# A hybrid SSD, pooling and gated-MLP block on one core: a low part behind dt's reading, row norm squares behind the panel's last put, and the last half stored in five chunks

## Chip, cores and metric

The kernel runs on one core of one Trainium2 chip. The metric is the device time of one execution in microseconds; the median over the runs is compared. Five engines work side by side, each through its own row of instructions in a fixed order: TensorE (PE; its weight loads are listed apart as PEld), VectorE (DVE), ScalarE (ACT), GpSimd (POOL) and SyncE (SP), which issues most of the DMAs.

## What is computed

One encoder block over 256 tokens of 2048 features in float32. Cut to what matters:

```python
hn = rmsnorm(h, mix_norm_pre)
z, xbc, dt_raw, u = jnp.split(hn @ w_in, split_at, axis=-1)     # 1024, 1536, 32, 1024 columns
y_ssd = ssd_mixer(z, xbc, dt_raw, ...)      # conv, softplus(dt_raw + dt_bias), a scan in both directions, gated by z
y_pool = pool_mixer(u, pool_w, pool_scale)  # centred means over 2, 4, 8, 16 tokens minus u, a linear map per group
h = h + rmsnorm(jnp.concatenate([y_ssd, y_pool], -1) @ w_out, mix_norm_post)

gate, val = jnp.split(rmsnorm(h, ffn_norm_pre) @ w_up, 2, axis=-1)          # 5632 columns each
ff = (gelu(dwconv_centred(gate, conv_w, conv_b)) * val) @ w_down
h = h + rmsnorm(ff, ffn_norm_post)

gate = sigmoid(rmsnorm(h, ple_norm_pre) @ w_ple_gate)
out = h + rmsnorm(gate * (p @ w_ple), ple_norm_post)
```

## The kernel before

**Matmuls in parts.** Each float32 operand is written as a sum of two parts in a shorter format, high and low, and a product is taken as high x high + high x low + low x high. `split` makes the parts of a weight tile: ACT casts the high part (line 151), VectorE subtracts it from the source to get the low one (line 152). `put` does so for activations, with a scale: ACT writes the high part (line 196), VectorE the low (line 197). All matmuls of such products are issued on line 87, so they are told apart by their tiles: the names `whi` and `wlo` at the end of a tile's name are the parts, the number ahead of them (0 or 1) is the half of a loaded 1 MB raw tile.

**Stages.** In order: `dtu` (dt and the pool branch's u, token-major, into three pairs of accumulators); `xbc` in slabs 2, 0, 1 (`feature_major`: four raw tiles each, two halves of 1024 columns, each half split and then multiplied); z, the scan and the pool mixer; `wo`, the output projection; the up projection of the MLP in 44 tiles, `ug` for gate and `uv` for value columns (`feature_pairs`, accumulators `ga` and `va`, of which a tile's first half goes high parts first and its second low parts first); the down projection `dn` in blocks, some of them by a scheme of seven products with sums stored to memory; the gate `gt` with the per-layer embedding `ple`, and the last addition and stores.

**Accumulators.** They live in PSUM. The pool `pmain` has six banks that the names take in turn, `pmisc` two. An accumulator of xbc takes a bank of dtu once that has been read out, in whichever order the pool hands them on. In the dtu stage each token half t is read by four instructions: dt on VectorE (line 540), u in three pieces on ACT (541), VectorE (542) and ACT (544). `rx` is the row factor of the first norm.

**What sets the order.** The code is recorded and its instructions are placed in each engine's row by a scheduler; `tc.issue_after(i)` puts what is recorded inside it behind instruction i in that order. Raw tiles (`raw`, four buffers) are loaded by SP (line 118) as soon as a buffer is free, so a load waits for the last reading of the tile four loads back. The dictionary `held` carries an instruction to the place where something is to be issued behind it. Before the change it is used in the up projection's first tile `ug00`, whose parts are made behind the panel's puts:

```python
behind = held.pop((name, u, j), None)
with tc.issue_after(behind) if behind else nullcontext():
    tiles.append(split(parts(f"{name}{u}_{j}"), r[:, j * 1024:(j + 1) * 1024], 0, 1024))
```

**Between wo and up.** `sublayer` ends by adding to the residual h in four column pieces; behind each piece `panel_part` transposes h on TensorE (`woxt`, line 383) and writes it back with `put` into the pages `wox`, which are the activations of up. Each page holds four of the sixteen feature blocks. Then `ple(0)` computes half of the embedding's product (`pl`, line 901), and `row_rstd("rf", h)` squares and sums each row half of h on ACT (`rfj`, line 399, 2048 columns), from which POOL makes the row factors `rf`. These are turned along the tokens by TensorE (`rfbp`) and multiplied in behind the first tiles of up.

**The end.** For the second token half, the last gate piece (`gtz`, 256 columns) is turned into a sum of squares; `rest_of` and `finish(1)` make the row factor `go1r` on POOL (line 1059), VectorE adds to h in four pieces of 512 columns (line 1064), and each is stored by SP (line 1066) as soon as it is done.

Of the kernel before, what the change touches and what calls it, by code (L numbers as in the profile page):

```python
# [11 lines left out]
F32 = mybir.dt.float32  # L12
F32R = mybir.dt.float32r
AF = mybir.ActivationFunctionType
ALU = mybir.AluOpType
# [36 lines left out]
def build(nc, a, out):  # L52
# [5 lines left out]
    with tile.TileContext(nc) as tc, \  # L58
# [9 lines left out]
        def ins(r):  # L68
            return getattr(r, "ins", r)

        def page(name, dtype=F32):
            return gp.tile([P, 2048], dtype, tag="pg", bufs=14, name=name)
# [4 lines left out]
        def tiny(name, n=2):  # L77
            return sp.tile([P, n], F32, tag="tiny", bufs=40, name=name)

        def main(name):  # L80
            return [pm.tile([P, 512], F32, tag="main", name=f"{name}_{i}") for i in range(2)]

        def misc(name):
            return pc.tile([P, 512], F32, tag="misc", name=name)

        def mm(o, lhsT, rhs, start, stop):
            last["pe"] = ins(nc.tensor.matmul(o, lhsT, rhs, start=start, stop=stop, skip_group_check=True))  # L87
# [16 lines left out]
        acc, acc2 = [main(f"dtu{t}") for t in range(2)], main("dtu2")  # L104
# [8 lines left out]
        last = {}  # L113
# [20 lines left out]
        def vec(i):  # L134
            return xt[0][:, i:i + 1] if i < V_SCW else vt[:, i - V_SCW:i - V_SCW + 1]


        spare, ready, held, stored = {}, {}, {}, {}

        def parts(name):  # L140

            if name in spare:
                return spare.pop(name)
            return [wp.tile([P, 1088], F32R, tag=tag, bufs=5, name=f"{name}{tag}") for tag in ("whi", "wlo")]

        def split(dst, src, c0, *cuts):

            hi, lo = dst
            for c1 in cuts:
                s = slice(c0, c1)  # L150
                last["act"] = ins(nc.scalar.copy(hi[:, s], src[:, s]))
                last["dve"] = ins(nc.vector.tensor_sub(lo[:, s], src[:, s], hi[:, s].bitcast(F32)))  # L152
                c0 = c1
            return hi, lo

        def raw(name, src, a_, b_):
            r = wp.tile([P, 2048], F32, tag="raw", bufs=4, name=name)
            last["dma"] = load(r[:, :a_ * b_].rearrange("p (a b) -> p a b", a=a_), src, True)
            return r
# [33 lines left out]
        def put(dst, src, scale):  # L193

            hi, lo = dst
            return (ins(nc.scalar.activation(hi, src, AF.Identity, scale=scale)),
                    ins(nc.vector.scalar_tensor_tensor(lo, src, scale, hi.bitcast(F32),
                                                       op0=ALU.mult, op1=ALU.subtract)))
# [3 lines left out]
        def aside():  # L202

            for job in (work.pop(0) if work else ()):
                job()
# [98 lines left out]
        def feature_major(name, w, c0, get, acc):  # L304

            for u in range(4):
                r = raw(f"{name}r{u}", w[c0 // 128 + u].unsqueeze(1), 1, 2048)
                tiles = []

                def step(j, kk, f):  # L310
                    k = 4 * u + 2 * j + kk
                    (wh, wl), (xh, xl) = tiles[j], get(k)
                    s = slice(kk * 512 + f * P, kk * 512 + (f + 1) * P)
                    for q, (ww, xx) in enumerate(((wh, xh), (wh, xl), (wl, xh))):
                        mm(acc[f // 2][:, f % 2 * L:(f % 2 + 1) * L], ww[:, s], xx,
                           k == 0 and q == 0 and f % 2 == 0, k == NK - 1 and q == 2)

                for j in range(2):
                    tiles.append(split(parts(f"{name}{u}_{j}"), r[:, j * 1024:(j + 1) * 1024], 0, 1024))
                    if u < 3:  # L320
                        for kk in range(2):
                            for f in range(4):
                                step(j, kk, f)
                if u == 3:
                    for f in range(4):
                        for j in range(2):
                            for kk in range(2):
                                step(j, kk, f)
                aside()
# [35 lines left out]
        def rms(name, parts, scale, n=1, base=EPS):  # L365

            for i, q in enumerate(parts):
                m = tiny(f"{name}m{i}", n)
                nc.gpsimd.tensor_scalar(m, q, scale, base, op0=ALU.mult, op1=ALU.add)
                base = m  # L370
            r = tiny(f"{name}r", n)
            nc.gpsimd.tensor_tensor(r, m, mhalf[:, :n], op=ALU.pow)
            last["mean"] = m
            return r

        def panel_part(name, pan, src, vcol, k0, k1):

            first = None
            for k in range(k0, k1, 2):
                ps = misc(f"{name}t{k}")  # L380
                for j in range(2):
                    for t in range(2):
                        nc.tensor.transpose(ps[:, (2 * j + t) * P:(2 * j + t + 1) * P],
                                            src[t][:, (k + j) * P:(k + j + 1) * P], ident)
                for j in range(2):
                    done = put(pan(k + j), ps[:, j * L:(j + 1) * L], vec(vcol + k + j))
                    last["put"] = done[1]
                    first = first or done
            return first

# [2 lines left out]
        def row_rstd(name, src):  # L393

            r = []
            for t in range(2):
                q = tiny(f"{name}q{t}", 1)
                junk = page(f"{name}j{t}")
                nc.scalar.activation(junk, src[t], AF.Square, accum_out=q)
                r.append(rms(f"{name}{t}", [q], 1.0 / D))  # L400
                means[name, t] = last["mean"]
            return r
# [60 lines left out]
        for u in range(0, NK, 2):  # L463
            r = [wp.tile([P, 2048], F32, tag="raw", bufs=4, name=f"dtur{u}") if u else r0, page(f"dtur{u + 1}")]
# [33 lines left out]
        with tc.issue_after(half[0]), tc.issue_after(half[1]):  # L498
# [3 lines left out]
            rx = row_rstd("rx", xs_)  # L502
# [35 lines left out]
        ut = page("u")  # L538
        for t in range(2):
            nc.vector.scalar_tensor_tensor(dt[:, t, :], acc[t][0][:, :32], rx[t], dtb, op0=ALU.mult, op1=ALU.add)  # L540
            nc.scalar.activation(ut[:, t * 1024:t * 1024 + 320], acc[t][0][:, 32:352], AF.Identity, scale=rx[t])  # L541
            nc.vector.tensor_scalar(ut[:, t * 1024 + 320:t * 1024 + 672], acc[t][1][:, :352], rx[t], None,
                                    op0=ALU.mult)
            nc.scalar.activation(ut[:, t * 1024 + 672:(t + 1) * 1024], acc2[t][:, :352], AF.Identity, scale=rx[t])
        rxb = along_tokens("rxb", rx)

# [230 lines left out]
        for t in range(2):  # L777
# [13 lines left out]
            r = rms(f"yn{t}", [ss], rz[t][:, 1:2], n=2)  # L791
# [103 lines left out]
        def ple(half):  # L895
            pl = page(f"pl{half}")
            acc = [main(f"ple{half}{t}") for t in range(2)]
            token_major(f"ple{half}", w_ple, half * 1024, [0, 1], lambda k: (pth[:, k, :], ptl[:, k, :]), acc)
            for t in range(2):
                for n in range(2):  # L900
                    nc.scalar.activation(pl[:, t * 1024 + n * 512:t * 1024 + (n + 1) * 512], acc[t][n],
                                         AF.Copy, scale=0.5)
            return pl
# [5 lines left out]
        h = [page(f"h{t}") for t in range(2)]  # L909
# [4 lines left out]


        pl = [ple(0)]
        rf = row_rstd("rf", h)
        for t in range(2):
            nc.gpsimd.tensor_scalar(fmean[t], means["rf", t], EPS, None, op0=ALU.mult)
        away = {n: dp.tile([P, 2048], F32, name=f"{n}_away") for n in ("h0", "h1", "pl0")}  # L920
# [112 lines left out]
        h = hb  # L1033
# [22 lines left out]
        def finish(t):  # L1056
            if t:
                r = tiny("go1r", 1)
                nc.gpsimd.tensor_tensor(r, sq[t][-1], mhalf[:, :1], op=ALU.pow)
            else:  # L1060
                r = rms("go0", sq[t], 1.0 / D)
            for c in range(4):
                s = slice(c * 512, (c + 1) * 512)
                nc.vector.scalar_tensor_tensor(vg[t][:, s], vg[t][:, s], r, h[t][:, s],
                                               op0=ALU.mult, op1=ALU.add)
                nc.sync.dma_start(out[t * P:(t + 1) * P, s], vg[t][:, s])

        for half in range(2):
            acc = [main(f"gt{half}{t}") for t in range(2)]
# [9 lines left out]
            for t in range(2):  # L1079
                for n, (o, c0) in enumerate(columns(acc[t])):  # L1080
                    c1 = c0 + o.shape[-1]
                    c = slice(half * 1024 + c0, half * 1024 + c1)
# [4 lines left out]
                    if end:  # L1087
# [3 lines left out]
                                                   op0=ALU.add, op1=ALU.mult)  # L1091
# [74 lines left out]
```

## Time and profile before

| | us |
|---|---|
| three runs | 1116.17, 1116.26, 1116.42 |
| median | 1116.26 |
| profiled execution | 1116.42 |
| its span, first to last instruction | 1114.6 |
| TensorE busy | 1102.3 (99%) |
| VectorE busy | 834.0 (75%) |
| ACT busy | 685.7 (62%) |
| mean granted TensorE clock | 0.997 |

The profile records one execution; its own time is 1.8 us more than its span. In the rows below a time is microseconds from the start of the span. A timeline row gives start, duration, engine, line, operation, output and inputs with the shape and the count, and in brackets the engine's idle time before it and what ended that. A row with a count above one groups neighbours of the same kind: its duration is that of the whole group. TensorE's matmuls overlap, so the spacing of their starts, not the duration of one, is what it needs for each.

### The profile page before, as it was taken

How to read it: one execution, taken by the hardware profiler on the slowest of the kernel's cores; microseconds unless marked ns; L12 is line 12 of the kernel's file. 1: busy time of each engine (PE TensorE's matmuls, PEld its weight loads, DVE VectorE, ACT ScalarE, POOL GpSimd, SP SyncE). 2: the span in 40 equal slices, each digit the busy share in tenths (PEclk: the TensorE clock that was granted, in tenths of full speed). 3: DMA queues.
4: the chain of work that ended last, by engine and by line, in shares of the span. 5: the costliest groups of instructions: out<-in, count | busy, mean ns of one | idle time of the engine just before them, and what ended most of it. 6: DMA issues, size and time to landing. Idle time of an engine off the chain costs nothing.

```text
span 1114.6 us, 15675 instructions
## 1 busy us (share of the span) xinstructions
PE 1102.3 (99%) x6040; PEld 963.5 (86%) x6040; DVE 834.0 (75%) x1047; ACT 685.7 (62%) x1006; POOL 53.0 (5%) x80
## 2 busy tenths in 40 slices
PE   9999999999999999999999999999999999999996
PEld 9999988888788888888888888888888888887885
DVE  6668888879786866767767677676788788897574
ACT  6757876555775565565655655556566466657462
POOL 0300023100200000000000000000000000001001
PEclk9999999999999999999999999999999999999998
DMA  9944445656576877777787687675788779875632
GB/s 354 376 174 150 154 151 212 242 210 224 212 282 252 304 262 249 280 259 253 280 290 253 239 323 253 213 253 220 253 312 296 265 275 348 308 253 209 247 131 75
DMA packets 48970, 275.68 MB, mean 247 GB/s; under 512 B 5248, under 2 KB 8192, under 8 KB 21632
## 3 DMA queue, kind: packets, MB, share of 16 engines
q1 hardware_dynamic: 48608, 274.33, 67.9%
q8 instruction: 47, 0.77, 0.3%
q10 hardware_dynamic: 288, 0.36, 0.1%
q14 instruction: 27, 0.22, 0.1%
HBM read 251.86 MB, written 22.81 MB: 246 GB/s over the span
## 4 chain that ended last, share of the span: by engine, by line
PE 92%; DMA 3%; ACT 2%; issue 1%; DVE 1%; POOL 0%; SPq 0%; POOLq 0%; DVEq 0%; ACTq 0%
PE va L87 22%; PE ga L87 21%; PE dna L87 15%; PE gt L87 7%; PE woa L87 7%; PE xbc L87 6%; PE dns L87 5%; PE z L87 4%; DMA dtur<-w_dtu 2%; DMA x<-x 1%; PE wos L87 1%; PE yd L87 1%; PE pw L87 1%; PE ple L87 0%; PE seg L87 0%
## 5 line engine op out<-in xcount | busy, mean ns | idle before, releaser
L87 PE MATMUL ga<-wox,ug_0whi 128*128 128x512 f32 x352 | 87.7, 391 | 0.0
L87 PE MATMUL va<-wox,uv_0whi 128*128 128x512 f32 x352 | 87.6, 391 | 0.0
L87 PE MATMUL ga<-wox,ug_1whi 128*128 128x512 f32 x352 | 87.2, 389 | 0.0
L87 PE MATMUL va<-wox,uv_1whi 128*128 128x512 f32 x352 | 86.9, 389 | 0.0
L87 PEld LDWEIGHTS va<-wox,uv_1whi 128*128 128x128 f32 x352 | 66.1, 188 | 13.7
L87 PEld LDWEIGHTS ga<-wox,ug_1whi 128*128 128x128 f32 x352 | 66.0, 188 | 13.7
L87 PEld LDWEIGHTS va<-wox,uv_0whi 128*128 128x128 f32 x352 | 64.6, 188 | 12.4
L87 PEld LDWEIGHTS ga<-wox,ug_0whi 128*128 128x128 f32 x352 | 64.6, 188 | 12.3
L87 PE MATMUL ga<-wox,ug_1wlo 128*128 128x256 f32 x352 | 49.7, 283 | 0.9 <-DVE ug_1wlo L152 0.9
L87 PE MATMUL ga<-wox,ug_0wlo 128*128 128x256 f32 x352 | 49.5, 283 | 0.0
L87 PE MATMUL va<-wox,uv_1wlo 128*128 128x256 f32 x352 | 49.4, 283 | 0.0
L87 PE MATMUL va<-wox,uv_0wlo 128*128 128x256 f32 x352 | 49.2, 283 | 0.0
L87 PEld LDWEIGHTS ga<-wox,ug_0wlo 128*128 128x128 f32 x352 | 46.8, 191 | 1.8
L87 PEld LDWEIGHTS va<-wox,uv_0wlo 128*128 128x128 f32 x352 | 46.7, 191 | 1.7
L87 PEld LDWEIGHTS ga<-wox,ug_1wlo 128*128 128x128 f32 x352 | 45.4, 192 | 1.3 <-DVE ug_1wlo L152 1.3
L87 PEld LDWEIGHTS va<-wox,uv_1wlo 128*128 128x128 f32 x352 | 45.4, 192 | 0.0
L877 POOL TENSOR_SCALAR dnm<-dnq,fmean 128x1 f32<-128x1 f32 x2 | 0.6, 282 | 586.8 <-ACT dnj L874 586.8
L87 PE MATMUL xbc<-hnh,xb_0whi 128*128 128x256 f32 x96 | 27.6, 288 | 0.7 <-ACT u L541 0.7
L87 PE MATMUL xbc<-hnh,xb_1whi 128*128 128x256 f32 x96 | 27.3, 285 | 0.0
L87 PE MATMUL xbc<-hnl,xb_1whi 128*128 128x256 f32 x96 | 27.2, 283 | 0.0
L87 PE MATMUL xbc<-hnh,xb_1wlo 128*128 128x256 f32 x96 | 27.1, 283 | 0.0
L87 PE MATMUL xbc<-hnh,xb_0wlo 128*128 128x256 f32 x96 | 27.1, 282 | 0.0
(1668 smaller groups left out, 3096.5 us busy)
## 6 DMA issues: line engine op xcount, KB each, us to landing
dn0r<-w_ffn_down SPq DMA_DIRECT2D x15, 1024.0 KB, 5.9
dn1r<-w_ffn_down SPq DMA_DIRECT2D x15, 1024.0 KB, 5.0
br<-w_ffn_down SPq DMA_DIRECT2D x14, 1024.0 KB, 4.9
bm<-block SPq DMA_DIRECT2D x14, 1024.0 KB, 4.8
zr<-w_z SPq DMA_DIRECT2D x8, 1024.0 KB, 4.9
wo0r<-w_out SPq DMA_DIRECT2D x8, 1024.0 KB, 4.8
gt0r<-w_ple_gate SPq DMA_DIRECT2D x8, 1024.0 KB, 4.8
gt1r<-w_ple_gate SPq DMA_DIRECT2D x8, 1024.0 KB, 4.9
```

The lines of the kernel that those rows point to most:

```text
L87: last["pe"] = ins(nc.tensor.matmul(o, lhsT, rhs, start=start, stop=stop, skip_group_check=True))
L877: nc.gpsimd.tensor_scalar(m, q, 1.0 / D, mean[t], op0=ALU.mult, op1=ALU.add)
```

## The change

Three edits.

A. `split` takes an instruction `behind` which the low part, but not the high part, is issued behind; `feature_major` looks one up in `held`. The dtu stage puts VectorE's reading of u for the first token half there, under the key of xbc's first raw tile (slab 2, tile 0), second half.

B. `panel_part` also notes the last high part, and the row norm `rf` of h is recorded behind it.

C. The second token half's last addition and its stores are cut at columns 256, 768, 1280 and 1792: chunks of 256, 512, 512, 512 and 256 instead of four of 512.

```diff
-        def split(dst, src, c0, *cuts):
+        def split(dst, src, c0, *cuts, behind=None):
 
             hi, lo = dst
             for c1 in cuts:
                 s = slice(c0, c1)
                 last["act"] = ins(nc.scalar.copy(hi[:, s], src[:, s]))
-                last["dve"] = ins(nc.vector.tensor_sub(lo[:, s], src[:, s], hi[:, s].bitcast(F32)))
+                with tc.issue_after(behind) if behind else nullcontext():
+                    last["dve"] = ins(nc.vector.tensor_sub(lo[:, s], src[:, s], hi[:, s].bitcast(F32)))
...
-                    tiles.append(split(parts(f"{name}{u}_{j}"), r[:, j * 1024:(j + 1) * 1024], 0, 1024))
+                    tiles.append(split(parts(f"{name}{u}_{j}"), r[:, j * 1024:(j + 1) * 1024], 0, 1024,
+                                       behind=held.pop((name, u, j), None)))
...
-                    last["put"] = done[1]
+                    last["put_high"], last["put"] = done
...
-            nc.vector.tensor_scalar(ut[:, t * 1024 + 320:t * 1024 + 672], acc[t][1][:, :352], rx[t], None,
-                                    op0=ALU.mult)
+            turned = ins(nc.vector.tensor_scalar(ut[:, t * 1024 + 320:t * 1024 + 672], acc[t][1][:, :352], rx[t], None,
+                                                 op0=ALU.mult))
+            held.setdefault(("xb2", 0, 1), turned)
...
-        rf = row_rstd("rf", h)
+        with tc.issue_after(last["put_high"]):
+            rf = row_rstd("rf", h)
...
-            for c in range(4):
-                s = slice(c * 512, (c + 1) * 512)
+            cuts = (0, 256, 768, 1280, 1792, 2048) if t else (0, 512, 1024, 1536, 2048)
+            for c0, c1 in zip(cuts, cuts[1:]):
+                s = slice(c0, c1)
```

Lines behind the edits move down by one to five in the changed kernel. The rows of instructions show what the edits move. VectorE at the first xbc tile, before (`xb_0wlo` and `xb_1wlo` are the low parts of the two halves of the raw tile `xb2r`, `dtu` the accumulators of the stage before):

```order
L152 TENSOR_TENSOR pooll<-poolw_602,poolh 128x1024
L152 TENSOR_TENSOR xb_0wlo<-xb2r_664,xb_0whi 128x1024
L152 TENSOR_TENSOR xb_1wlo<-xb2r_664,xb_1whi 128x1024
L540 SCALAR_TENSOR_TENSOR dt<-dtu_0_90,rx0r,small 128x32
L542 TENSOR_SCALAR u<-dtu_1_91,rx0r 128x352
L540 SCALAR_TENSOR_TENSOR dt<-dtu_0_92,rx1r,small 128x32
L542 TENSOR_SCALAR u<-dtu_1_93,rx1r 128x352
```

The same engine at the same place, after:

```order
L153 TENSOR_TENSOR pooll<-poolw_602,poolh 128x1024
L153 TENSOR_TENSOR xb_0wlo<-xb2r_664,xb_0whi 128x1024
L542 SCALAR_TENSOR_TENSOR dt<-dtu_0_90,rx0r,small 128x32
L544 TENSOR_SCALAR u<-dtu_1_91,rx0r 128x352
L153 TENSOR_TENSOR xb_1wlo<-xb2r_664,xb_1whi 128x1024
L542 SCALAR_TENSOR_TENSOR dt<-dtu_0_92,rx1r,small 128x32
L544 TENSOR_SCALAR u<-dtu_1_93,rx1r 128x352
```

The second half's low part has moved behind dt and u of the first token half. With that, TensorE's first matmul into the second xbc accumulator waits for VectorE, and before for ACT. TensorE's row itself is the same there; before:

```order
L87 MATMUL xbc_0_662<-hnh_118,xb_0wlo 128x256 [waits DVE_49]
L87 MATMUL xbc_0_662<-hnh_118,xb_0whi 128x256
L87 MATMUL xbc_0_662<-hnl_120,xb_0whi 128x256
L87 MATMUL xbc_0_662<-hnh_118,xb_0wlo 128x256
L87 MATMUL xbc_1_663<-hnh_118,xb_0whi 128x256 [waits Activation_49]
L87 MATMUL xbc_1_663<-hnl_120,xb_0whi 128x256
```

And after:

```order
L87 MATMUL xbc_0_662<-hnh_118,xb_0wlo 128x256 [waits DVE_49]
L87 MATMUL xbc_0_662<-hnh_118,xb_0whi 128x256
L87 MATMUL xbc_0_662<-hnl_120,xb_0whi 128x256
L87 MATMUL xbc_0_662<-hnh_118,xb_0wlo 128x256
L87 MATMUL xbc_1_663<-hnh_118,xb_0whi 128x256 [waits DVE_49]
L87 MATMUL xbc_1_663<-hnl_120,xb_0whi 128x256
```

The bank of the second accumulator has become that which VectorE's u empties.

ACT between wo and up, before (`pl` is the embedding's product, `rfj` the squares of the row norm, `wox` the last page's high part, `uv` a value tile, `gr` a copy of gate sums):

```order
L901 ACTIVATE pl_2961<-ple_1_2965 128x512
L399 ACTIVATE rfj_3005,rfq_3004<-h_2156 128x2048
L196 ACTIVATE wox_2880<-woxt_2952,vt 128x256
L399 ACTIVATE rfj_3012,rfq_3011<-h_2157 128x2048
L151 CAST ug_1whi<-ug01r_3198 128x1024
L151 CAST uv_0whi<-uv00r_3276 128x1024
L151 CAST uv_1whi<-uv00r_3276 128x1024
L362 COPY gr_3060<-ga_0_3061 128x256
L362 COPY gr_3060<-ga_1_3062 128x256
```

After:

```order
L904 ACTIVATE pl_2961<-ple_1_2965 128x512
L197 ACTIVATE wox_2880<-woxt_2952,vt 128x256
L401 ACTIVATE rfj_3005,rfq_3004<-h_2156 128x2048
L401 ACTIVATE rfj_3012,rfq_3011<-h_2157 128x2048
L151 CAST ug_1whi<-ug01r_3198 128x1024
L151 CAST uv_0whi<-uv00r_3276 128x1024
L364 COPY gr_3060<-ga_0_3061 128x256
L364 COPY gr_3060<-ga_1_3062 128x256
L151 CAST uv_1whi<-uv00r_3276 128x1024
```

The last high part stands ahead of both squares, and two copies of gate sums ahead of a cast. On TensorE three of the eight matmuls `ga<-wox,ug_1whi` of the second gate tile, which before stand ahead of the first gate tile's eight `ug_1wlo`, now follow that tile's last ones:

```order
L87 MATMUL ga_0_3154<-wox_2878,ug_1whi 128x512
L87 MATMUL ga_1_3155<-wox_2878,ug_1whi 128x512
L87 MATMUL ga_0_3154<-wox_2878,ug_1whi 128x512
L87 MATMUL ga_0_3061<-wox_2880,ug_1wlo 128x256
L87 MATMUL ga_1_3062<-wox_2880,ug_1wlo 128x256
```

This is the changed kernel's row: the group ends after five of its eight. Nothing else moves but edit C's additions and stores.

## Prediction

> **What bounds the kernel now.** I read the profile from the top down: the busy shares and the chain that ended last, then TensorE's own list of waits, then the stretches around the three edits instruction by instruction.
>
> ```profile
> PE 1102.3 (99%) x6040; PEld 963.5 (86%) x6040; DVE 834.0 (75%) x1047; ACT 685.7 (62%) x1006; POOL 53.0 (5%) x80
> PE 92%; DMA 3%; ACT 2%; issue 1%; DVE 1%; POOL 0%; SPq 0%; POOLq 0%; DVEq 0%; ACTq 0%
> ```
>
> TensorE is busy 99% of the span and carries 92% of the chain. Faster vector work buys nothing by itself; only a place where TensorE stands still, and the tail after its last matmul, can be shortened. Its list of waits from 52 us to the end is short:
>
> ```profile
> PE ga L87 <- DVE ug_1wlo L152: 0.9, 1, 0.9
> PE xbc L87 <- ACT u L541: 0.7, 1, 0.7
> PE dnxt L383 <- DVE h_back L888: 0.3, 1, 0.3
> PE woxt L383 <- DVE h L888: 0.3, 1, 0.3
> ```
>
> Each line is the waiting instruction, what released it, total us, times, longest. The first two are the places of edits B (the row norm) and A (the low part of xbc's second half tile); edit C (five stores) lies in the tail. All the waits that are left to win are 2.2 us, so no large result is possible either way unless a new wait arises.
>
> **Edit A, the first xbc tile.** The timeline there (start, duration, engine, line, operation, idle before it and releaser):
>
> ```profile
> 50.72 1.22 DVE L152 TENSOR_TENSOR xb_0wlo<-xb2r,xb_0whi 128x1024 fp32r<-128x1024 f32 x1
> 51.86 1.22 DVE L152 TENSOR_TENSOR xb_1wlo<-xb2r,xb_1whi 128x1024 fp32r<-128x1024 f32 x1
> 52.87 0.28 PE L87 MATMUL xbc<-hnh,xb_0wlo 128*128 128x256 f32 x1
> 52.99 0.25 DVE L540 SCALAR_TENSOR_TENSOR dt<-dtu,rx0r,small 128x32 f32<-128x32 f32 x1
> 53.10 0.33 SPq L118 DMA_DIRECT2D xb0r<-w_xb  x1
> 53.16 0.58 DVE L542 TENSOR_SCALAR u<-dtu,rx0r 128x352 f32<-128x352 f32 x1
> 53.27 0.53 ACT L541 ACTIVATE u<-dtu,rx0r 128x320 f32<-128x320 f32 x1 [1.65 <-DVE dt L540]
> 53.65 0.24 DVE L540 SCALAR_TENSOR_TENSOR dt<-dtu,rx1r,small 128x32 f32<-128x32 f32 x1
> 53.86 0.39 PE L87 MATMUL xbc<-hnh,xb_0whi 128*128 128x256 f32 x1 [0.70 <-ACT u L541]
> 54.08 0.28 PE L87 MATMUL xbc<-hnl,xb_0whi 128*128 128x256 f32 x1
> 54.20 0.28 PE L87 MATMUL xbc<-hnh,xb_0wlo 128*128 128x256 f32 x1
> 56.35 0.28 PE L87 MATMUL xbc<-hnh,xb_1wlo 128*128 128x256 f32 x1
> 64.83 1.04 ACT L151 CAST xb_0whi<-xb0r 128x1024 fp32r<-128x1024 f32 x1 [1.77 <-PE xbc L87]
> ```
>
> The seventh xbc matmul (53.86) opens a second accumulator and needs a bank of the dtu stage to be read out. The reader is ACT's u at 53.27, which waits for VectorE's dt, and dt stands behind two low parts. After the edit VectorE goes from xb_0wlo straight to dt and u of the first token half, then to xb_1wlo, and the row order gives the second accumulator the bank that VectorE's u releases. By the spacing of the rows (51.86 − 50.72 = 1.14 for a low part, 0.17 for dt): dt starts at 51.86, u at 52.03 and ends at 52.61, and TensorE may go at about 52.66. It arrives, at one matmul per 0.12 us (54.08 to 54.20), at 52.99, so 0.3 us of slack is left. Without the wait the eighth matmul starts at 53.11 instead of 54.08: gain 0.97 us. That is more than the listed 0.70 because the first matmul after the wait runs 0.22 instead of 0.12 and its weight load had to come too.
>
> What is moved is paid for elsewhere. xb_1wlo starts behind u, at 52.5, and ends at 53.73 instead of 53.08; its first reader stands at 56.35 before and would stand at 55.38, so 1.6 us cover it. The load of xb0r waits for that low part's raw tile and is issued 0.65 us later (53.75); its first reader, the ACT cast at 64.83 (63.86 after), waits there for TensorE and not for the load, over 10 us behind the issue. The second token half's dt starts where it did, 53.65: the same three operations lie before it. Cost of the move: nothing that reaches TensorE.
>
> **Edit B, up's first tiles.**
>
> ```profile
> 298.38 0.87 DVE L197 SCALAR_TENSOR_TENSOR wox<-woxt,vt,wox 128x256 fp32r<-128x256 f32 x2
> 299.30 1.97 ACT L399 ACTIVATE rfj<-h 128x2048 f32<-128x2048 f32 x1
> 300.58 1.98 PE L87 MATMUL ga<-wox,ug_1whi 128*128 128x512 f32 x8
> 301.19 0.53 ACT L196 ACTIVATE wox<-woxt,vt 128x256 fp32r<-128x256 f32 x1
> 301.75 0.48 DVE L197 SCALAR_TENSOR_TENSOR wox<-woxt,vt,wox 128x256 fp32r<-128x256 f32 x1 [2.51 <-ACT wox L196]
> 302.15 1.22 DVE L152 TENSOR_TENSOR ug_1wlo<-ug00r,ug_1whi 128x1024 fp32r<-128x1024 f32 x1
> 303.42 1.21 PE L87 MATMUL ga<-wox,ug_1wlo 128*128 128x256 f32 x8 [0.87 <-DVE ug_1wlo L152]
> 304.47 2.00 PE L87 MATMUL ga<-wox,ug_0whi 128*128 128x512 f32 x8
> 308.10 0.65 ACT L362 COPY gr<-ga 128x256 f32<-128x256 f32 x2 [0.29 <-PE ga L87]
> 315.62 0.49 PE L87 MATMUL rfbp<-ident,rfbw 128*128 128x128 f32 x3
> ```
>
> Here a 2 us square over a row half (rfj, 299.30) stands on ACT before the panel's last high part (wox, 301.19). VectorE waits 2.51 us for that, the low part of ug behind it comes late, and TensorE stands. After the edit the high part takes rfj's place: 299.30 to 299.83. VectorE, idle since 299.25, follows as it does now 0.56 us after ACT's start (301.75 − 301.19), at 299.86; ug_1wlo 0.40 later, at 300.26; TensorE 1.27 after that (303.42 − 302.15), at 301.53.
>
> TensorE's arrival: the eight ug_1whi matmuls take (1.98 − 0.39)/7 = 0.227 us each, the eight ug_1wlo 0.12 each, as the xbc matmuls of the same width above. Undisturbed, the sixteen would put the next group, ug_0whi, at 300.58 + 1.82 + 0.96 = 303.36 instead of 304.47: gain 1.11 us. But three of the eight ug_1whi matmuls now stand later in the row, so TensorE comes to the low part after five, at 301.71. That leaves 0.18 us, and its weight load, one matmul ahead, asks at about 301.49: up to 0.05 us may be lost, and I keep 1.08.
>
> Behind it: the first rfj starts 0.5 us later and the second ends when it did, since ACT has the same three operations in another order. Its result is turned by TensorE at 315.62 (rfbp), 12 us later and 11 us after the gain. The two copies of ga (gr, 308.10) now stand ahead of a cast of the first value tile on ACT instead of behind it, and wait for TensorE there (0.29 us now); the cast comes a microsecond or two later, and the value tiles are read only behind rfbp, past 315.6. The three moved ug_1whi matmuls follow the first gate tile's last ones, so that tile is summed 0.7 us sooner in the row; no matmul is added.
>
> **Edit C, the last half's stores.**
>
> ```profile
> 1103.67 0.43 DVE L1090 SCALAR_TENSOR_TENSOR gth<-gth,pl 128x256 f32<-128x256 f32 x1 [1.24 <-ACT gth L1089]
> 1108.23 2.74 DVE L1064 SCALAR_TENSOR_TENSOR vg<-vg,go1r,h_back 128x512 f32<-128x512 f32 x4 [0.81 <-POOL go1r L1059]
> 1109.01 2.32 SPq L1066 DMA_DIRECT2D out<-vg  x4
> 1111.00 0.33 SPq L1066 DMA_DIRECT2D out<-vg  x1
> DMA to landing us min/median/max: 2.5/2.8/2.8
> ...
> 1109.40:1109.80 0.40, 0.00 (x0) 0.00 (x0) 0.40 (x2) 0.00 (x0) 0.00 (x0) 0.50 0.00 0
> 1110.20:1112.20 2.00, 0.00 (x0) 0.00 (x0) 0.77 (x2) 0.00 (x0) 0.00 (x0) 0.50 1.04 339
> 1109.40:1113.40 4.00, 0.00 (x0) 0.00 (x0) 1.57 (x3) 0.00 (x0) 0.00 (x0) 0.50 0.80 262
> ```
>
> The last two columns of the window rows are the DMA share and GB/s. Nothing moves until 1109.8, 0.8 us behind the first issue; then the sixteen engines are full (1.04). The four stores need 0.80 x 4.00 = 3.2 us of full engines, 0.8 each, while they are issued only (1111.00 − 1109.01)/3 = 0.66 apart. So it is the engines and not VectorE that set the end from the second store on, and 0.15 us of backlog builds per store.
>
> With a first chunk of 256 columns, VectorE is done after about 0.43 us (row 1103.67) instead of 0.75: first issue near 1108.70, data from 1109.5. That is 0.4 us of work, then the engines run dry until the second chunk, issued 0.66 later at 1109.37, flows at 1110.17. From there 0.8 x 3 + 0.4 = 2.8 us of work: end of data at 1112.97, against 1109.8 + 3.2 = 1113.0. By that the gain is 0.03 us. If instead the last issue sets the end, five operations end 0.1 us later than four, and the last store carries half the bytes: 0.4 − 0.1 = 0.3 gained. If a chunk with 1 KB rows costs as much as one with 2 KB rows, the backlog grows by 0.4 less the earlier start: about 0.3 lost. I take 0.05, near the first reading, since the engines' share shows them full, and keep −0.3 to +0.3.
>
> The Trainium skill has two rules on that. "Perfetto Trace Analysis", section DMA Optimizations, says splitting may let the whole finish sooner if the engines are generally idle, and that transfers under 2 KB carry overhead. This trace shows the engines full at 1.04, so its condition is not met here. "DMA: Bandwidth & Descriptors", Anatomy of one DMA, gives a fixed 2.0 us plus bytes over 436 GB/s (fitted to another issue path): an estimate by it makes a 128 KB store 0.3 us shorter than a 256 KB one, and with the last issue 0.1 later the sum would be 2.25 us: 1114.0, between the forecast and the third rival below.
>
> **Sum.** 0.97 + 1.08 + 0.05 = 2.1 us. The profiled execution took 1116.42 us, 1.8 more than its span; it would be 1114.3. It stands 0.16 above the median of the three runs, 1116.26, from which the forecast is 1114.1. A difference under 0.2%, 2.2 us, is about what a measurement of this kernel can't tell from none, and its edge is 1114.0: the forecast lies at it, just inside.
>
> **The rivals.**
>
> *Given back in the down projection.* A gain lasts only if nothing with a clock of its own stands downstream. TensorE's next waits are the small ones of the list, released by chains that TensorE starts itself. The nearest thing to a free clock is this:
>
> ```profile
> 815.16 1.22 DVE L218 TENSOR_TENSOR dn016f<-dn0r 128x1024 f32<-128x1024 f32 x1 [0.58 <-DMA dn0r<-w_ffn_down]
> 816.30 1.22 DVE L152 TENSOR_TENSOR dn_0wlo<-dn0r,dn_0whi 128x1024 fp32r<-128x1024 f32 x1
> 818.65 0.62 PE L87 MATMUL dna<-dn_0wlo,hidh 128*128 128x512 f32 x2
> ```
>
> VectorE waits for a load there, and the low part made behind it ends at 817.52, 1.13 us before TensorE reads it. If loads there do not move with TensorE, a shift of 2.05 us eats that slack and 0.9 us comes back: 1115.0. Against it: the loads are issued when VectorE and ACT release their tiles, and those follow TensorE, so the load should come earlier too. 0.15.
>
> *One of the two waits stays in another form.* In A VectorE's u need only be 0.33 us later than I have it, in B the low part 0.2. If one edit gives only half, the sum is about 1.5 to 1.6: 1114.7 to 1114.8; if B or A fails whole, 1115.2. 0.17.
>
> *The tail gives more, or the restarts cost more than I count.* Stores at +0.3 and the full 1.11 of B make 2.4: 1113.9 and, with a little of the other waits of the list, down to 1113.5. 0.15.
>
> *Slower: the moved low part becomes TensorE's wait.* xb_1wlo now stands behind dt and u, which themselves wait for the end of dtu's accumulation. If u came late, xb_1wlo would hold the twenty-seventh xbc matmul at 55.38. It has 1.6 us; to end slower than before by 0.2% it would have to be late by 1.6 + 2.1 + 2.2 us, nearly 6 us in all, and slower at all needs 3.7. Nothing in the rows delays dt except the low parts (ACT's u, released by it, waits 1.65 us for dt alone). 0.03.
>
> **How the numbers follow.** The forecast as worked out, 1113.8 to 1114.4 with its centre at 1114.1: 0.50. It lies on the edge, and I give half of it to each side. Faster by over 0.2%: 0.25 of that and 0.15 of the tail rival, 0.40. Within 0.2%: the other 0.25, 0.15 for the down projection and 0.17 for the wait that stays, 0.57. Slower: 0.03. The range takes in both partial rivals and the tail's better end: 1113.5 to 1115.3.
>
> **What would show it.** A right: the row of waits on ACT u (L541) is gone, TensorE's seventh xbc matmul starts at 52.99, xb_1wlo starts near 52.5. A wrong: a wait of xbc on VectorE's u, or on xb_1wlo. B right: the wait on ug_1wlo is gone or under 0.1, the wox high part stands ahead of both rfj, ug_1wlo starts near 299.3 (300.26 less A's 0.97). Both together: the first ga of the down projection starts 2.1 us sooner and the gap stays constant from 304 us to the last gt matmul; if it shrinks after 793, the first rival is right, and the row of the wait names the tile. C right: first store near 0.3 us sooner after go1r, last landing within 0.3 of the same distance from go1r. The prediction is wrong if TensorE's list of waits shows a new line over 0.3 us, or the tail from its last matmul to the end changes by more than 0.3 us.

## The result, and the profile after

| | before | after |
|---|---|---|
| median of 21 runs, us | 1116.39 | 1114.40 |
| range, us | 1115.99 to 1117.51 | 1113.95 to 1115.71 |
| profiled execution, us | 1116.42 | 1114.42 |
| its span, us | 1114.6 | 1112.6 |

The ratio is 0.9982, with a 95% interval from 0.9976 to 0.9988: 2.0 us faster, where 2.1 were forecast from a median that the later runs put 0.13 us higher. The time, 1114.4, lies 0.3 above the forecast and inside the range. The interval leaves out "no change", so a difference just under 0.2% can be told from none here, which the forecast had doubted.

TensorE's list of waits, from 50 us on, has lost both places. Its columns are as before: who waited, for whom, us in total, times, longest.

```profile
PE dnxt L385 <- DVE h_back L891: 0.3, 1, 0.3
PE woxt L385 <- DVE h L891: 0.3, 1, 0.3
```

The first xbc matmul before the change, and the timeline at that tile after it:

```profile
52.20 0.36 PE L87 MATMUL xbc<-hnh,xb_0whi 128*128 128x256 f32 x1
```

```profile
51.50 0.24 DVE L542 SCALAR_TENSOR_TENSOR dt<-dtu,rx0r,small 128x32 f32<-128x32 f32 x1
51.66 0.57 DVE L544 TENSOR_SCALAR u<-dtu,rx0r 128x352 f32<-128x352 f32 x1
52.16 1.22 DVE L153 TENSOR_TENSOR xb_1wlo<-xb2r,xb_1whi 128x1024 fp32r<-128x1024 f32 x1
52.51 0.36 PE L87 MATMUL xbc<-hnh,xb_0whi 128*128 128x256 f32 x1
53.31 0.28 PE L87 MATMUL xbc<-hnh,xb_0whi 128*128 128x256 f32 x1
53.40 0.33 SPq L118 DMA_DIRECT2D xb0r<-w_xb  x1
55.71 0.28 PE L87 MATMUL xbc<-hnh,xb_1wlo 128*128 128x256 f32 x1
```

The seventh matmul (53.31) follows the sixth without a pause, and the moved low part is done at 53.38, 2.3 us before its first reading at 55.71. From the first matmul to that reading it is 3.20 us, and before it was 56.35 − 52.20 = 4.15: the 0.95 us of the forecast. But the first matmul itself starts at 52.51 here and started at 52.20 there, ahead of anything that the edits touch. So the reading is only 0.64 us earlier. The experiments show where the rest went.

Between wo and up:

```profile
298.08 1.12 PE L87 MATMUL ga<-wox,ug_0wlo 128*128 128x256 f32 x8
298.65 0.53 ACT L197 ACTIVATE wox<-woxt,vt 128x256 fp32r<-128x256 f32 x1
299.62 1.22 DVE L153 TENSOR_TENSOR ug_1wlo<-ug00r,ug_1whi 128x1024 fp32r<-128x1024 f32 x1
299.96 1.30 PE L87 MATMUL ga<-wox,ug_1whi 128*128 128x512 f32 x5
301.11 1.12 PE L87 MATMUL ga<-wox,ug_1wlo 128*128 128x256 f32 x8
314.25 2.07 PE L87 MATMUL va<-wox,uv_0whi 128*128 128x512 f32 x8
```

VectorE's ug_1wlo starts 0.97 us behind the last high part, as worked out, and is done 0.27 us before TensorE reads it. That reading is at 301.11, where five undisturbed matmuls would bring it (299.96 + 5 x 0.227 = 301.10). From the first reading of xb_1wlo to the first value matmul it is 314.25 − 55.71 = 258.54 us; before it was 315.98 − 56.35 = 259.63, by the rows shown there and the value matmul's:

```profile
315.98 0.94 PE L87 MATMUL va<-wox,uv_0whi 128*128 128x512 f32 x3
1105.72 0.28 PE L87 MATMUL gtz<-gt_1whi,dnxl 128*128 128x256 f32 x1
```

That is 1.09 us gained. The last matmul stands at 1105.72 in this trace and after the change at

```profile
1104.02 0.28 PE L87 MATMUL gtz<-gt_1whi,dnxl 128*128 128x256 f32 x1
```

so 789.74 and 789.77 us lie between: nothing of the gain is given back on the way, the down projection included. The tail after the change (additions, stores, and a window row with the DMA share and GB/s last):

```profile
1106.54 2.87 DVE L1069 SCALAR_TENSOR_TENSOR vg<-vg,go1r,h_back 128x256 f32<-128x256 f32 x5 [0.81 <-POOL go1r L1063]
1107.05 2.82 SPq L1071 DMA_DIRECT2D out<-vg  x5
1108.30:1108.50 0.20, 0.00 (x0) 0.00 (x0) 0.20 (x2) 0.00 (x0) 0.00 (x0) 1.00 0.08 21
1107.71:1111.71 4.00, 0.00 (x0) 0.00 (x0) 1.70 (x3) 0.00 (x0) 0.00 (x0) 0.64 0.72 262
```

The first store comes 0.51 instead of 0.78 us behind the additions' start, and the engines do run dry after it (0.08). But the same 1 MB took 0.72 x 4.00 = 2.9 us of full engines instead of 3.2. From the additions' start to the end of the span it is 1112.6 − 1106.5 = 6.1 us instead of 6.4: 0.3 gained, where 0.05 was forecast. The forecast had named a tail that changes by more than 0.3 us, counted from the last matmul, as a sign of being wrong. It went from 1114.6 − 1105.7 = 8.9 to 1112.6 − 1104.0 = 8.6, which is right at that limit.

### The profile page after: what moved, and what is told of

The parts are those of the page before. It is cut to its first block, busy times and chain, and to the rows that moved or that the text cites. A ratio compares the mean times of both kernels' runs of the same rounds, so it can differ in the third digit from the quotient of the medians.

```text
span 1112.6 us, 15677 instructions
## 1 busy us (share of the span) xinstructions
PE 1102.0 (99%) x6040; PEld 963.9 (87%) x6040; DVE 834.0 (75%) x1048; ACT 685.6 (62%) x1006; POOL 53.9 (5%) x80
## 4 chain that ended last, share of the span: by engine, by line
PE 97%; DMA 1%; DVE 0%; ACT 0%; issue 0%; POOL 0%; POOLq 0%; DVEq 0%; ACTq 0%
PE ga L87 22%; PE va L87 22%; PE dna L87 15%; PE gt L87 7%; PE woa L87 7%; PE xbc L87 6%; PE dns L87 5%; PE z L87 4%; PE dtu L87 4%; DMA dtur<-w_dtu 1%; PE wos L87 1%; PE yd L87 1%; PE pw L87 1%; PE ple L87 0%; PE woxt L385 0%
```

## Experiments

In all of them the distances are: from the first xbc matmul to the first reading of xb_1wlo (A), from there to the first value matmul (B), and from the first last-addition of the second half to the end of the span (C). Each edit alone and the shorter tail were run eleven times. The other experiments were run once, so only distances within their traces are compared.

### Each edit alone

```diff
 a_only: without B and C
-        with tc.issue_after(last["put_high"]):
-            rf = row_rstd("rf", h)
+        rf = row_rstd("rf", h)
-            cuts = (0, 256, 768, 1280, 1792, 2048) if t else (0, 512, 1024, 1536, 2048)
+            cuts = (0, 512, 1024, 1536, 2048)
 b_only: without A (below) and C (as above)
-            held.setdefault(("xb2", 0, 1), turned)
 c_only: without A and B (as above)
```

> Edit A alone. Theory (three independent gains, A's being the time that TensorE stood for ACT's u): from the first xbc matmul to the first that reads xb_1whi 2.96 us, as in the changed kernel, instead of 3.91; the wait on u is gone; the end 0.95 us sooner than before, ratio 0.9991; the waits of up's first tiles and the tail as before. Rival (the 0.31 us by which the first xbc matmul came later in the changed kernel's profile, 52.51 against 52.20, is a price of A): first xbc matmul again near 52.5, and only 0.64 us of net gain, ratio 0.9994. Rival 2 (the shift is given back before the end): same first numbers, ratio 1.000.

> Edit B alone. Theory: VectorE's ug_1wlo starts 0.97 us after the last wox high part starts, TensorE's wait for it is gone, and the stretch from the gate tile's ug_0wlo group to its ug_0whi group takes 3.98 us instead of 5.78, of which 0.68 are the three matmuls that moved: 1.12 us gained, and the end 1.1 us sooner, ratio 0.9990. Rival (given back in the down projection where VectorE waits for a load): the first value matmul 1.1 us sooner, but the last gate matmul less than 0.6 us sooner.

> Edit C alone. From the first of the last additions' start to the end of the span: 6.41 us before, 6.06 in the changed kernel. Theory (the last store's issue and size set the end, since data flow at the rate that the stores come): 6.0 to 6.1, the end 0.3 us sooner, ratio 0.9997. Rival, which is the prediction's own first reading (the engines are full from the second store on, and the first chunk's head start is lost in the gap behind it): 6.35 to 6.4, and the changed kernel's 6.06 was a lucky rate of the engines.

| | time, us | ratio, 95% interval | first xbc matmul | A | B | C |
|---|---|---|---|---|---|---|
| before | 1116.33 | | 52.20 | 4.15 | 259.63 | 6.4 |
| A alone | 1115.88 | 0.9995 (0.9986 to 1.0004) | 52.56 | 3.20 | 259.63 | 6.4 |
| B alone | 1115.29 | 0.9991 (0.9982 to 0.9999) | 52.91 | 3.19 | 258.55 | 6.4 |
| C alone | 1116.11 | 0.9997 (0.9988 to 1.0006) | 52.84 | 3.43 | 259.61 | 6.1 |
| all three | 1114.40 | 0.9982 (0.9976 to 0.9988) | 52.51 | 3.20 | 258.54 | 6.1 |

The medians fall by 0.45, 1.04 and 0.22 us, 1.7 together, and by 2.0 with all three; the intervals of single edits are too wide to say more, and those of A and C include no change. The traces are sharper. B gives 1.08 to 1.12 wherever it is (1.12 in the trace of the shorter tail below), and C 0.3. Nothing is given back later by any of the three: from the first value matmul to the last matmul it is 789.7 to 789.8 us in each. A was expected to give 0.95, and as a distance it does, 3.20. But with B alone, in which edit A is undone, that distance is 3.19 too, and TensorE doesn't wait for u at all. So the size of A is in question. The rival for A, that the late first matmul is a price of the edit, falls with the same row: it is latest, 52.91, without A.

### What the wait on u is made of

The kernel before, profiled once more:

> The kernel before once more, for its start. Theory (two clocks: TensorE's arrival at the first xbc matmul and VectorE's at dt both vary from one execution to the next, and the wait on u is their difference): the first xbc matmul starts somewhere from 52.2 to 52.9, dt from 52.6 to 53.8, and the distance from the first xbc matmul to the first reading of xb_1wlo is 3.2 plus whatever dt is late, not 4.15 again except by chance. Rival (the 0.95 us wait belongs to the kernel before and the smaller ones to the other builds): 52.2, 4.15.

```profile
52.42 0.36 PE L87 MATMUL xbc<-hnh,xb_0whi 128*128 128x256 f32 x1
52.84 0.24 DVE L540 SCALAR_TENSOR_TENSOR dt<-dtu,rx0r,small 128x32 f32<-128x32 f32 x1
53.70 0.39 PE L87 MATMUL xbc<-hnh,xb_0whi 128*128 128x256 f32 x1 [0.33 <-ACT u L541]
```

The same instructions, and the wait is 0.33 instead of 0.70. Nine profiles of kernels in which edit A is undone (the other experiments below are among them) give the rule. Up to 50 us the instructions stand in the same order in all nine:

| profile | first xbc matmul | dt starts | dt behind it by | A's distance above 3.20 |
|---|---|---|---|---|
| B alone | 52.91 | 52.57 | −0.34 | 0 |
| C alone | 52.84 | 52.92 | 0.08 | 0.23 |
| small chunks first | 52.74 | 52.99 | 0.25 | 0.40 |
| small chunks last | 52.56 | 52.91 | 0.35 | 0.50 |
| before, again | 52.42 | 52.84 | 0.42 | 0.57 |
| shifted stores | 52.41 | 52.87 | 0.46 | 0.62 |
| C's sizes, even places | 52.58 | 53.29 | 0.71 | 0.87 |
| before | 52.20 | 52.99 | 0.79 | 0.95 |
| half square | 52.70 | 53.80 | 1.10 | 1.26 |

The loss is dt's lateness plus 0.15 to 0.16 us in every one in which there is a loss. So it is a race of two chains of work: the arrival of TensorE's wanders by 0.7 us over these profiles, that of VectorE's by 1.2. VectorE's hangs on ACT's: in all nine, dt starts 13.2 us after ACT's square of x, by rows like these (before, then half square):

```profile
39.77 1.91 ACT L399 ACTIVATE rxj<-x 128x2048 f32<-128x2048 f32 x1
```

```profile
40.58 1.91 ACT L402 ACTIVATE rxj<-x 128x2048 f32<-128x2048 f32 x1
53.80 0.25 DVE L543 SCALAR_TENSOR_TENSOR dt<-dtu,rx0r,small 128x32 f32<-128x32 f32 x1
54.66 0.39 PE L87 MATMUL xbc<-hnh,xb_0whi 128*128 128x256 f32 x1 [1.00 <-ACT u L544]
```

With the edit dt starts 12.1 us after that square (51.50 − 39.41 in the changed kernel, and the same in three more profiles), sooner by one low part, and none of these has a wait on u. The mean of the nine losses is 0.60 us, which is an estimate of what A is worth on the average; the profile shown before the change had the second largest. What moves the two chains in the first 40 us was not traced.

### The low part far too late

The prediction's slower rival, provoked: the low part is put behind a step in the middle of softplus, with B and C undone.

```diff
-            held.setdefault(("xb2", 0, 1), turned)
...
-        nc.vector.tensor_mul(e1, e1, e2)
+        held["xb2", 0, 1] = ins(nc.vector.tensor_mul(e1, e1, e2))
```

> Edit A with the low part placed much further back, behind the middle of the softplus chain, so that VectorE makes it near 56.2 to 57.4 us. This is the prediction's slower rival, provoked. Theory: the wait on u is gone as with A, but TensorE waits for xb_1wlo instead, 1.3 to 1.6 us, and the end is 1.3 to 1.6 later than with A alone, 0.8 to 1.1 later than before. Rival (the low part has more room than that, since the row puts other matmuls ahead): no wait, time as with A alone.

```profile
56.35 1.22 DVE L153 TENSOR_TENSOR xb_1wlo<-xb2r,xb_1whi 128x1024 fp32r<-128x1024 f32 x1
57.62 0.39 PE L87 MATMUL xbc<-hnh,xb_1wlo 128*128 128x256 f32 x1 [1.73 <-DVE xb_1wlo L153]
```

TensorE waits 1.73 us, A's distance is 5.33 instead of 3.20, and the span is 1115.8, 1.7 longer than with A alone, whose first xbc matmul came 0.27 later; its one run took 1117.61. The mechanism is that of the rival and the size a little more than expected. Placed as edit A has it, the low part starts 4.2 us earlier than this and has 2.3 to spare.

### The length of the square

A, B and C are undone, and the first of the two squares leaves out half of its columns.

```diff
-                nc.scalar.activation(junk, src[t], AF.Square, accum_out=q)
+                sw = slice(0, 1024 if name == "rf" and t == 0 else 2048)
+                nc.scalar.activation(junk[:, sw], src[t][:, sw], AF.Square, accum_out=q)
```

> Edit B undone, A and C too, but the first square of the row norm goes over 1024 of the 2048 columns (half of that sum is left out). Theory (the wait is the length of the square that stands ahead of the last high part): the high part starts 0.9 to 1.0 us sooner, the stretch from the first ug_0wlo matmul to the first value matmul falls from 21.1 to 20.1 to 20.2 (19.9 with B), and TensorE's wait for ug_1wlo from 0.87 to 0.1 or less. Rival (the gain came with the other moves of B: the three matmuls and the copies): the stretch stays at 21.1.

```profile
299.53 1.12 PE L87 MATMUL ga<-wox,ug_0wlo 128*128 128x256 f32 x8
300.14 1.11 ACT L402 ACTIVATE rfj<-h 128x1024 f32<-128x1024 f32 x1
301.18 0.53 ACT L197 ACTIVATE wox<-woxt,vt 128x256 fp32r<-128x256 f32 x1
301.41 1.98 PE L87 MATMUL ga<-wox,ug_1whi 128*128 128x512 f32 x8
303.41 1.22 PE L87 MATMUL ga<-wox,ug_1wlo 128*128 128x256 f32 x8
```

Before, the group that stands first there is

```profile
298.69 1.11 PE L87 MATMUL ga<-wox,ug_0wlo 128*128 128x256 f32 x8
```

The square takes 1.11 instead of 1.97 us, and the high part starts 0.85 sooner relative to TensorE (301.18 − 299.53 = 1.65 behind this group, before 301.19 − 298.69 = 2.50). The low part's group starts at 303.41 where undisturbed it would at 303.23 (301.41 + 8 x 0.227), so 0.2 us of the wait is left, where 0.1 or less was expected. B's distance is 315.97 − 57.16 = 258.81 (57.16 is the first reading of xb_1wlo there): 0.82 of B's 1.08 us come from 0.86 us of ACT's time alone. (The distances of 21.1 and 20.1 in the expectation were taken from a matmul at the edge of a window, which is not the same one in each trace; from the group of eight it is 17.3 before, 16.2 with B and 16.4 here.) The moved matmuls and copies aren't needed for these 0.82 us; the other 0.26 were not divided between them and the rest of the square.

### Which stores are slow

Four patterns of the second half's stores, with A and B undone:

```diff
-            cuts = (0, 256, 768, 1280, 1792, 2048) if t else (0, 512, 1024, 1536, 2048)
 c_last
+            cuts = (0, 512, 1024, 1536, 1792, 2048) if t else (0, 512, 1024, 1536, 2048)
 c_first
+            cuts = (0, 256, 512, 1024, 1536, 2048) if t else (0, 512, 1024, 1536, 2048)
 c_shift
+            cuts = (0, 768, 1280, 1792, 2048) if t else (0, 512, 1024, 1536, 2048)
 c_even: C's sizes, other places
+            cuts = ((0, 256), (512, 1024), (1024, 1536), (1536, 2048), (256, 512)) if t else ...
```

> Only the last of the four stores cut in two: chunks of 512, 512, 512, 256 and 256 columns; everything else as before. Same stretch, 6.41 before. Theory (the last store's size sets the end): the last issue comes 0.1 later than before, its landing takes 2.2 instead of 2.8: 5.9 to 6.05. Rival (full engines set the end, and the first store's start counts): 6.4.

> Edit C's first cut alone: chunks of 256, 256, 512, 512 and 512 columns; the rest as before. Stretch from the first last-addition to the end of the span: 6.37 before, 6.11 with C, 6.93 with the small chunks last. Theory 1 (what counts is that the stores' data do not pile up: the lead of a small first chunk leaves the engines a pause, and each later store lands in 2.2 us instead of 2.8): last issue 2.85 us after the start, landing 2.2 to 2.3 later, end 0.9 after that: 5.95 to 6.1. Theory 2 (where the pieces begin counts: pieces of 2 KB that begin at odd multiples of 1 KB are written faster than those at even ones): the last three stores land in 2.8 as before, 6.45 to 6.6.

> Four stores, shifted: chunks of 768, 512, 512 and 256 columns, so the three later ones begin where edit C's do, but the first is large and late. Same stretch. Theory 1 (no pile-up): the first issue comes at 1.1 instead of 0.8 us, the stores follow at 0.66 and pile up as before: landing 2.8, 6.5 or more. Theory 2 (where pieces begin): landing 2.2, last issue near 2.85, 5.95 to 6.1.

> Edit C alone with the same five sizes in the same order (256, 512, 512, 512, 256 columns), but the three pieces of 512 begin at columns 512, 1024 and 1536, multiples of 2 KB, and the last 256 columns are 256 to 511. Only the places differ from C. Theory 2 (where the pieces begin): the middle stores land in 2.5 to 2.8 instead of 2.1 to 2.2, and the stretch from the first last-addition to the end is 6.4 to 6.6. Theory 1 (the pause that the small first chunk leaves): 6.05 to 6.15, as C.

Window rows of the same stretch, from 2.8 to 4.4 us behind the additions' start: before, C alone, shifted, and C's sizes at even places.

```profile
1111.03:1112.63 1.60, 0.00 (x0) 0.00 (x0) 0.00 (x0) 0.00 (x0) 0.00 (x0) 0.50 1.05 325
```

```profile
1110.99:1112.59 1.60, 0.00 (x0) 0.00 (x0) 0.07 (x1) 0.00 (x0) 0.00 (x0) 0.57 1.01 370
```

```profile
1110.85:1112.45 1.60, 0.00 (x0) 0.00 (x0) 0.00 (x0) 0.00 (x0) 0.00 (x0) 0.53 1.00 368
```

```profile
1111.36:1112.96 1.60, 0.00 (x0) 0.00 (x0) 0.07 (x1) 0.00 (x0) 0.00 (x0) 0.50 1.06 327
```

| stores (columns) | the 512s begin at | GB/s, 2.8 to 4.4 us | 256 KB to landing, median us | C's distance, us |
|---|---|---|---|---|
| before: 512 x4 | 0, 2, 4, 6 KB | 325 | 2.8 | 6.4 |
| small chunks last: 512 x3, 256 x2 | 0, 2, 4 KB | 312 | 2.7 | 6.9 |
| small chunks first: 256 x2, 512 x3 | 2, 4, 6 KB | 333 | 2.7 | 6.6 |
| C's sizes, even places | 2, 4, 6 KB | 327 | 2.7 | 6.6 |
| shifted: 768, 512 x2, 256 | 3, 5 KB | 368 | 2.5 | 6.15 |
| C: 256, 512 x3, 256 | 1, 3, 5 KB | 370 | 2.2 | 6.1 |

The engines are full in all of them (1.00 to 1.07), so they set the rate, and not the issues. In this stretch the stores whose 512-column pieces begin at odd multiples of 1 KB in the 8 KB rows run at 368 to 370 GB/s, and those at even ones at 312 to 333. The other profiles fit: 320 to 325 in five more with four stores of 512, 369 in the changed kernel, 358 with the shorter tail below, whose 512s begin at 1, 3 and 5 KB. The last pair decides: C and C's sizes at even places have the same five sizes in the same order at the same spacing, and differ only in the columns, and the second loses all of the gain and 0.2 more. Already the first store of 512 columns, behind the same pause, differs: it lands in 2.2 us with C and in 2.5 at the even place. The third lands in 2.2 against 2.8, and the last, of 128 KB, in 2.2 against 2.7. The rate isn't one number per place, though: in the 0.8 us just ahead of the stretch both kernels of the pair write 371 GB/s. The first theory (the pause that a small first chunk leaves) fails at this pair and at the small chunks first, the theory tried with the small chunks last (the last store's size) at 6.9 where 6.0 was expected. The theory of the places had the shifted stores land in 2.2 us; they took 2.4 to 2.5, and their distance is a little over the 6.1 expected. Why the place matters isn't shown. A piece is read from the same columns of the tile in SBUF as it is written to in the row in memory, so these runs don't tell either which of the two sides counts.

### A shorter tail

```diff
 on the changed kernel: pieces 0-256, 256-768, 1792-2048, 768-1280, 1280-1792, the stores in that order
+                if t and c0 == 1792:
+                    nc.scalar.activation(vg[t][:, s], vg[t][:, s], AF.Identity, scale=r)
+                    nc.gpsimd.tensor_add(vg[t][:, s], vg[t][:, s], h[t][:, s])
```

> The changed kernel with a shorter tail: of the second token half's last addition, columns 1792 to 2047 are done by ACT (times the row factor) and GpSimd (plus h), both idle there, and stored third; VectorE does 256, 512, 512, 512. Theory (the last issue sets the end): VectorE is done 0.4 us sooner, last issue 2.5 instead of 2.9 us after the start, landing in 2.3 to 2.5: the stretch falls from 6.06 to 5.7 to 5.9, the time 0.2 to 0.35 us under the changed kernel's, ratio to before 0.998. Rival (the engines are full again, or GpSimd slows VectorE): 6.0 to 6.2, no gain.

```profile
1106.27 2.94 DVE L1073 SCALAR_TENSOR_TENSOR vg<-vg,go1r,h_back 128x256 f32<-128x256 f32 x4 [0.80 <-POOL go1r L1063]
1106.86 1.14 POOL L1071 TENSOR_TENSOR vg<-vg,h_back 128x256 f32<-128x256 f32 x1 [0.62 <-ACT vg L1070]
L1073 DVE SCALAR_TENSOR_TENSOR vg<-vg,go1r,h_back 128x512 f32<-128x512 f32 x3 | 2.5, 897 | 0.0
```

The last row groups the three pieces of 512 columns (busy us, mean ns of one, idle before). The longest of them, and the three in the changed kernel:

```profile
1107.34 1.21 DVE L1073 SCALAR_TENSOR_TENSOR vg<-vg,go1r,h_back 128x512 f32<-128x512 f32 x1
```

```profile
L1069 DVE SCALAR_TENSOR_TENSOR vg<-vg,go1r,h_back 128x512 f32<-128x512 f32 x3 | 2.1, 746 | 0.0
```

VectorE has 256 columns less to do and takes 0.07 us longer (2.94 against 2.87): its three 512-column pieces last 897 instead of 746 ns in the mean, 0.45 us together, with GpSimd's addition beside them. One piece bears all of it: the one that starts at 1107.34, while that addition is running, takes 1.21 us, and the other two take no longer than without it. The last issue comes at 1109.24, 2.97 us behind the additions' start, as late as in the changed kernel. The rival's half of it is right: the neighbour costs VectorE what it saves. The Trainium skill's "SBUF — State Buffer", section Who interferes with whom, says that a VectorE instruction with two inputs in SBUF contends with a GpSimd instruction that reads SBUF. The trace agrees: both are of that kind, and the pieces lose 0.45 beside a 1.14 us addition. The tail is 5.97 instead of 6.09 us nevertheless (by the spans to a hundredth, 1112.24 and 1112.63), with its stores landing in 1.9 to 2.1 us instead of 1.9 to 2.2. The median is 1114.22, the ratio to before 0.9980 (0.9971 to 0.9989), against 0.9982 (0.9976 to 0.9988) for the change itself; the two can't be told apart.

## Why the prediction was right, and where it was not

The sum of 2.1 us stands against 2.0 measured, but two of its three terms were off, A's by 0.37 too much in the mean and C's by 0.25 too little, and made up for each other. That the total fits so closely is luck. With the sizes that the runs show it is 0.60 + 1.09 + 0.3 = 2.0. (The sum of the forecast, taken from 1116.26, gives 1114.2 and not 1114.1.)

- **Edit A, 0.97.** The mechanism was right: dt behind two low parts, ACT's u behind dt, TensorE behind u; after the edit the wait is gone, the moved low part has 2.3 us to spare, and the load of xb0r has no effect. The size failed at the step "without the wait the eighth matmul starts at 53.11": true of that one execution and taken for the kernel. Over nine profiles the wait costs 0 to 1.26 us, 0.60 in the mean; the median of the runs with A alone falls by 0.45.
- **Edit B, 1.08.** Right in mechanism and size: 1.08 to 1.12 in three traces, 0.82 from a square shortened by half. The loss of up to 0.05 that was allowed for TensorE's weight load asking early can't be seen: the low part is done 0.27 us before its reading.
- **Edit C, 0.05.** Wrong by 0.25 at the step "3.2 us of full engines, 0.8 each": that price was taken from stores at multiples of 2 KB, and the edit moved them to places where the same bytes take less, 0.72 x 4.00 = 2.9 us of full engines instead of 3.2. The gap behind the first chunk was there as predicted. That the full engines set the end was right too; the time that I took as fixed was not. The forecast's other reading, in which the last issue sets the end, has the number 0.3, but not the reason: the last store, with half the bytes, takes 2.2 us to land as the full ones do. An estimate by the Trainium skill's "DMA: Bandwidth & Descriptors", Anatomy of one DMA, makes a 128 KB store 0.3 us shorter than one of 256 KB. In C alone that holds for the first store, 1.9 us against 2.1 to 2.2 for the 256 KB ones, and not for the last, 2.2, on which the end hangs.
- **Given back in the down projection.** No: 789.7 us from the first value matmul to the last matmul before, and the same after. The place is real, though. In the second profile of the kernel before, the load that the forecast names landed later: VectorE waited 1.61 us for it, and TensorE's first two matmuls on the low part behind it took 0.70 instead of 0.62 us. A load of the same kind 26 us later cost more:

```profile
816.04 1.23 DVE L218 TENSOR_TENSOR dn016f<-dn0r 128x1024 f32<-128x1024 f32 x1 [1.61 <-DMA dn0r<-w_ffn_down]
841.66 1.23 DVE L218 TENSOR_TENSOR dn026f<-dn0r 128x1024 f32<-128x1024 f32 x1 [1.99 <-DMA dn0r<-w_ffn_down]
844.08 0.74 PE L87 MATMUL dna<-dn_0wlo,hidh 128*128 128x512 f32 x2 [0.18 <-DVE dn_0wlo L152]
```

  In that trace the stretch takes 790.3 us, 0.6 more, some 0.5 of it at the second place. The kernel is the same, so it comes and goes with the execution.
- **One wait stays, or the tail gives more.** No wait stays: both are gone from TensorE's list. The tail did give the 0.3 of that rival, but A's smaller worth took it away again.
- **Slower by a late low part.** Its mechanism works (1.73 us of wait when provoked), and edit A stays 2.3 us away from it.

The ratio, 0.9982, lies just inside 0.2%, where the forecast had it, and its interval reaches over that edge.

## What to carry to other kernels

A wait that is the difference of two chains that wander has no single size: profile the kernel more than once, or read both arrivals and their spread, before taking the idle time of one trace as the gain. When a long instruction stands ahead of a short one that another engine waits for, the gain of swapping them can be read from one trace, if all that follows hangs on the same chain: here 1.08 us were worked out and 1.08 to 1.12 measured. And with full DMA engines, changing where the pieces of a store begin can matter more than how many there are: here the same five sizes ended 0.5 us apart.

## What was not expected of the hardware

Over the same 1.6 us of the tail, stores of 2 KB pieces into rows of 8 KB ran at 358 to 370 GB/s where the pieces begin at odd multiples of 1 KB and at 312 to 333 GB/s at even ones, with the same sixteen engines full. And two chains at the start of the kernel, ACT's and TensorE's, shift against one another by up to 1.4 us between executions (dt from 0.34 us ahead of the first xbc matmul to 1.10 behind it).
